# Sums of FFN weights formed in DRAM by accumulating transfers instead of by GpSimd in SBUF

## The chip, the cores and the metric

One core of one Trainium2 chip runs the program alone. The metric is device time in microseconds (us). The kernel before takes 1333.62 us, the median of three runs that lie between 1332.47 and 1334.59. The profile below is of one more execution, which took 1331.28 us.

## The reference, cut to what matters

Everything is float32. A decoder block of 1024 tokens and width 1024 computes two branches (sliding-window attention and an mLSTM), merges them, and then runs the feed-forward network (FFN), whose inner width is 2816. The change is in the FFN:

```python
x = x + (sigmoid(ga) * ya + sigmoid(gm) * ym) @ w_out     # branches, merged
f = rmsnorm(x, norm2_g)
x = x + (silu(f @ w_ffn_gate) * (f @ w_ffn_up)) @ w_ffn_down
return rmsnorm(x, final_norm_g)
```

w_ffn_gate and w_ffn_up are 1024 x 2816, w_ffn_down is 2816 x 1024.

## The kernel before

**Products in parts.** TensorE multiplies float32 as three passes over rounded halves: an operand is split into a rounded part `hi` (ScalarE copy) and the rest `lo` (VectorE subtraction), the helper `split` (L72, L73), and a product is hi·hi + hi·lo + lo·hi. A `whi` or `wlo` tile is such a half of a weight block of 128x512; five of each rotate.

**Seven products for eight.** The three matrix products of the FFN are cut into 2x2 blocks and done with the seven products of the Strassen-Winograd scheme. Products 1, 2 and 4 take a block of the weight as it is; products 5, 6, 7 and 3 take the sums x21+x22, x21+x22+x11, x11+x21 and x12+(x21+x22+x11) (the signs are folded into the other operand). `ORDER` and `SEQ` (L784 to L787) list the gate and up products: n runs over 22 panels (11 pairs of gate and up), i over the seven products, and each product is 12 matmuls of 128x512. In the projection down (`DORD`, L949) the seven products run one after the other, each over 11 chunks p of 12 matmuls.

**Where the sums are made.** `load_pair` brings a panel's raw blocks x11, x12, x21, x22 from `w_gu` by SP's queue; `prep` (L806 to L826) has GpSimd add two of them into a tile `s_` where product i needs a sum (L813) and splits it. `prep` runs LA = 4 products ahead of TensorE. In the projection down `dprep` (L981 to L998) does the same with tiles `lz` that `dload` has brought; GpSimd adds into `sT` or into the right half of `ld`, and for products 5 and 6 ScalarE copies `sT` into `ld`. The left half of `ld` is a combination of hidden activations (`hd_` in DRAM, stored by `h_store`).

**What sets the order.** Instructions of one engine run in the order in which the framework put them; DMAs are issued by SP's queue, also in order, so that a DMA which waits for a buffer or for data holds all that stand behind it. GpSimd (POOL) also makes one half of the activation sums `f_t` (L768), the activation `w` (L921) and the sums `hs` of hidden activations (L877).

**Stages in time.** Branches up to about 327 us; the attention projection (`w_br`, L665 to L668, result `mg`) from there; the mLSTM output gates (`sg`, L676 to L683); the merge; the projection `w_out` (j = 0 to 7, 12 us each, from 561 us); gate and up from 657 us; down until the end.

Of the kernel before, what the change touches and what calls it, by code (L numbers as in the profile page):

```python
# [9 lines left out]
F32 = mybir.dt.float32  # L10
F32R = mybir.dt.float32r
AF = mybir.ActivationFunctionType
ALU = mybir.AluOpType
PSUM = bass.MemoryType.PSUM

P = 128
S = 1024
D = 1024
FF = 2816
KD = D // P  # L20
NF = FF // P
NT = S // P
HALF = 512
EPS = 1e-6
# [5 lines left out]


@with_exitstack
def hybrid_block(ctx, tc, xT, xt, par, g3row, cst, abias, w_fm, w_mv, w_br, w_o, w_gu, w_dn, out):
    nc = tc.nc
    V, A, G, T = nc.vector, nc.scalar, nc.gpsimd, nc.tensor

# [4 lines left out]
    wp = ctx.enter_context(tc.tile_pool(name="wp", bufs=1))  # L41
    wk = ctx.enter_context(tc.tile_pool(name="wk", bufs=3))
    sm = ctx.enter_context(tc.tile_pool(name="sm", bufs=2))
# [7 lines left out]
    def blk(name, dtype=F32, n=1024):  # L51
        return sb.tile([P, n], dtype, name=name, tag="blk", bufs=NB)
# [18 lines left out]
    def split(hi, lo, src, eng=V):  # L71
        A.activation(hi, src, AF.Copy)  # L72
        eng.tensor_tensor(lo, src, hi.bitcast(F32), ALU.subtract)  # L73
# [40 lines left out]
    def hs(h):  # L114
        return slice(h * HALF, (h + 1) * HALF)
# [62 lines left out]
    for k in range(KD):  # L178
        xr = xrs[k]
        h_, l_ = blk("uh", F32R), blk("ul", F32R)  # L180
        g = prm[:, C_G1 + k:C_G1 + k + 1]
# [238 lines left out]
    mg = []  # L420
# [212 lines left out]
    run(gai, 16)  # L633


    ph_a.close()
    lo_eng[0] = V
    ph_b = ExitStack()
# [24 lines left out]
    for j in range(KD):  # L663
        wt = weights(w_br[j], 4)
        A.activation(mg[j], mg[j], AF.Sigmoid)  # L665
        for h in range(2):
            ps = proj(wt, o_, 4, h)
            V.tensor_tensor(mg[j][:, hs(h)], ps, mg[j][:, hs(h)], ALU.mult)  # L668


    hs_ = [[None, None], [None, None]]
    for i in range(4):
        wt = weights(w_fm[18 + i], KD)
        for h in range(2):
            if i % 2 == 0:
                hs_[h][i // 2] = (pv2(blk2("hh", F32R)), pv2(blk("hl", F32R)))  # L676
            sg = work("sg")
            gate(sg, wt, h)
            for q in range(2):
                V.scalar_tensor_tensor(sg[:, q * 256:(q + 1) * 256],  # L680
                                       hT[h * 2 + q][:, i * 256:(i + 1) * 256], prm[:, C_GM + i:C_GM + i + 1],
                                       sg[:, q * 256:(q + 1) * 256], ALU.mult, ALU.mult)
            hi, lo = (b[:, i % 2] for b in hs_[h][i // 2])  # L683
            split(hi, lo, sg)
    h_ = lambda k, h: tuple(b[:, k % 2] for b in hs_[h][k // 2])

# [65 lines left out]
    def halves(t):  # L752
        return t[:, 0:HALF], t[:, HALF:1024]
# [17 lines left out]
    def half(name, tag, bufs):  # L771
        return pC.tile([P, HALF], F32, name=name, tag=tag, bufs=bufs)
# [9 lines left out]


    ORDER = (1, 6, 5, 7, 2, 3, 4)  # L784
    NP2 = NF // 2
    SEQ = [(n, i) for i2 in ((1, 5), (6, 7), (2, 3, 4)) for n in range(2) for i in i2]
    SEQ += [(n, i) for n in range(2, 2 * NP2) for i in ORDER]  # L787
    LA = 4
    raws, hl, sums = {}, {}, {}

    def load_pair(n):

        raws[n] = [x for i in range(2) for x in pair_raw(n, i)]

    def pair_raw(n, i):
        if n == 0 and i == 1:
            r = [half("wr", "ev", 6) for _ in range(2)]
            for k in range(2):
                nc.sync.dma_start(out=r[k], in_=w_gu[n, i, :, hs(k)])
            return r  # L800
        r = blk("wr2") if i else wp.tile([P, 1024], F32, name="wraw", tag="wraw", bufs=2)
        nc.sync.dma_start(out=r, in_=w_gu[n, i])
        return halves(r)

    def prep(g):
        n, i = SEQ[g]  # L806
        if n and i == 6 and n + 1 < 2 * NP2:
            load_pair(n + 1)
        x11, x12, x21, x22 = raws[n]

        def s_(k, a, b):
            sums[n, k] = half("s_", "ws", 5)
            G.tensor_tensor(sums[n, k], a, b, ALU.add)  # L813
        if i in (5, 6) and (n, 5) not in sums:
            s_(5, x21, x22)
        if i == 6:
            s_(6, sums[n, 5], x11)
        elif i == 7:
            s_(7, x11, x21)
        elif i == 3:  # L820
            s_(3, x12, sums[n, 6])
        src = {1: x11, 2: x12, 4: x22}
        hi = wp.tile([P, HALF], F32R, name="whi", tag="whi", bufs=5)
        lo = wp.tile([P, HALF], F32R, name="wlo", tag="wlo", bufs=5)
        split(hi, lo, src[i] if i in src else sums[n, i])
        hl[n, i] = (hi, lo)  # L826

    later = []
    for j in range(KD):
        wt = weights(w_o[j], KD)  # L830
        xr = wp.tile([P, 1024], F32, name="xr2", tag="wraw", bufs=2)
        nc.sync.dma_start(out=xr, in_=xT[j])
        xc = blk("xc")
        f = blk("f")
        F_.append(f)
        g = prm[:, C_G2 + j:C_G2 + j + 1]
        if j == KD - 1:
            load_pair(0)
            prep(0)
            prep(1)  # L840
        for h in range(2):
            ps = proj(wt, m_, KD, h)
            V.tensor_tensor(xc[:, hs(h)], ps, xr[:, hs(h)], ALU.add)
            A.activation(f[:, hs(h)], xc[:, hs(h)], AF.Copy, scale=g)
            later.append((xc, j, h))
            if len(later) > 1:
                to_tokens(*later.pop(0))
        if j % 2 == 1 and j < 6:
            f_even(j // 2)
        elif j == 6:  # L850
            f_split(1, 3, F_[6][:, 0:HALF])
# [81 lines left out]
            if i == 4 and s == 1:  # L933
                h_sums(n // 2, sg)

    load_pair(1)

    def f_rest(i, kt):
        (z11, z12), (z21, z22) = halves(F_[2 * kt]), halves(F_[2 * kt + 1])
# [9 lines left out]
    DORD = (1, 5, 2, 3, 6, 7, 4)  # L949
    NC_ = 7 * NP2  # L950
    LD, LP = 6, 4
    draw, dop, sT, dtm = {}, {}, {}, {}

    def t_at(p):
        if (p // 2) not in sT:
            sT[p // 2] = blk("sT")
        return halves(sT[p // 2])[p % 2]

    def dload(c):

        i, p = DORD[c // NP2], c % NP2
        t = blk("ld")
        draw[c] = t
        nc.sync.dma_start(out=t[:, 0:HALF], in_=hd_[i - 1, p])

        def ld(k, j, dst=None):
            dst = half("lz", "ev", 6) if dst is None else dst
            nc.sync.dma_start(out=dst, in_=w_dn[2 * p + k, :, hs(j)])
            return dst
        z = t[:, HALF:1024]  # L970
        if i in (1, 2, 3):
            ld(*{1: (0, 0), 2: (1, 0), 3: (1, 1)}[i], z)
        elif i == 5:
            dtm[c] = ld(0, 0), ld(0, 1)
        elif i == 7:
            dtm[c] = ld(1, 1), ld(0, 1)
        elif i == 6:
            dtm[c] = (ld(1, 1),)
        else:
            dtm[c] = (ld(1, 0),)  # L980

    def dprep(c):
        i, p = DORD[c // NP2], c % NP2
        t = draw.pop(c)
        z, tm = t[:, HALF:1024], dtm.pop(c, None)
        if i == 5:
            G.tensor_tensor(t_at(p), *tm, ALU.add)
            A.activation(z, t_at(p), AF.Copy)
        elif i == 6:
            G.tensor_tensor(t_at(p), tm[0], t_at(p), ALU.add)  # L990
            A.activation(z, t_at(p), AF.Copy)
        elif i == 7:
            G.tensor_tensor(z, *tm, ALU.add)
        elif i == 4:
            G.tensor_tensor(z, tm[0], t_at(p), ALU.add)
        hi, lo = blk("xzh", F32R), blk("xzl", F32R)
        split(hi, lo, t)
        dop[c] = hi, lo  # L998

    z11, z12 = halves(F_[6])  # L1000
# [2 lines left out]
        f_rest(6, kt)  # L1003
    prep(2)
    prep(3)
    rest = [(i, kt) for i in (7, 2, 3, 4) for kt in range(4)]
    for g, (n, i) in enumerate(SEQ):
        if g + LA < len(SEQ):
            prep(g + LA)
        product7(n, i)  # L1010
        if g == 0:
            to_tokens(*later.pop(0))
            V.tensor_tensor(rstd2, ss2[:, 0], ss2[:, 1], ALU.add)
            rstd_of(rstd2, rstd2, D, NT)
        if n == 2 * NP2 - 1 and i in (7, 2, 3):
            for c in {7: range(LP), 2: range(2), 3: range(2, LP)}[i]:
                (dload if i == 7 else dprep)(c)
        for _ in range(2):
            if rest:
                f_rest(*rest.pop(0))  # L1020
# [95 lines left out]
def _layout(i):  # L1116
# [30 lines left out]
    def cols(w):  # L1147

        K, N = w.shape
        return np.ascontiguousarray(w.reshape(K // P, P, N // P, P).transpose(2, 1, 0, 3)).reshape(N // P, P, K)  # L1150
# [9 lines left out]
    w_br = np.concatenate([cols(wa), cols(a["w_mlstm_branch"][0])], axis=0)  # L1160
    w_o = cols(a["w_out"][0])

    w_gu = np.stack([cols(a[k][0]).reshape(NF // 2, 2, P, 4, 2, P).transpose(0, 1, 2, 4, 3, 5).reshape(NF // 2, 2, P, D)
                     for k in ("w_ffn_gate", "w_ffn_up")], axis=1).reshape(NF, 2, P, D)
    w_dn = a["w_ffn_down"][0].reshape(NF, P, D)
    return [xT, x.reshape(NT, P, D), par, np.tile(a["final_norm_g"][None, :], (P, 1)), cst, abias, w_fm, w_mv, w_br, w_o, w_gu, w_dn]


_NAMES = ["xT", "xt", "par", "g3row", "cst", "abias", "w_fm", "w_mv", "w_br", "w_o", "w_gu", "w_dn"]


# [15 lines left out]
```

## Time and profile before

| | |
|---|---|
| median of three runs | 1333.62 us |
| profiled execution | 1331.28 us |
| its span | 1329.5 us |
| TensorE busy | 1303.4 us (98%) |
| VectorE busy | 765.0 us (58%) |
| ScalarE busy | 572.7 us (43%) |
| GpSimd busy | 458.5 us (34%) |
| moved by DMA | 143.13 MB, mean 108 GB/s |

Engines: PE is TensorE, DVE VectorE, ACT ScalarE, POOL GpSimd, SPq the queue of DMAs that SyncE issues. A row of the chain or of a timeline names line, engine, operation, output and inputs, and behind a bracket the idle time ahead of it and what ended it. "PEclk" is the clock that TensorE was granted as a share of full speed (2.4 GHz; the other level is 1.2 GHz). A row for several instructions in a timeline ("x2") gives the time from the start of the first to the end of the last.

### The profile page before, as it was taken

To read this page: it belongs to the slowest core of one execution; us is meant where nothing else is said; L and a number is where in the kernel's file an instruction comes from. 1 tells how busy PE (TensorE), PEld (TensorE's weight loads), DVE (VectorE), ACT (ScalarE), POOL (GpSimd) and SP (SyncE) were. 2 spreads that over 40 slices of the span, in tenths; PEclk is the share of its full clock that TensorE was granted. 3 is DMA by queue.
4 is the path that set the end of the run, shared out by engine and by line. 5 is a ranking of instruction groups with operands and counts; after the bars stand their busy time and mean duration, and the time that the engine had idled before them with its cause. 6 is when DMAs were issued, how large, how long until landed. Compare 5 with 4: busy or idle time off the path is not lost.

```text
span 1329.5 us, 16764 instructions
## 1 busy us (share of the span) xinstructions
PE 1303.4 (98%) x6090; PEld 1066.1 (80%) x6090; DVE 765.0 (58%) x1261; ACT 572.7 (43%) x1078; POOL 458.5 (34%) x374
## 2 busy tenths in 40 slices
PE   8999999999999999999989999999999999999986
PEld 6888998777888888888778888888888888888865
DVE  5369764565535444433587555555556564664796
ACT  6369974566213222224453333333233344565333
POOL 0245443211000000010266657556655725600470
PEclk9999999999999999999989999999999999999989
DMA  9111011101111111224323321323232249983761
GB/s 338 48 57 39 17 33 48 49 9 33 56 48 42 44 48 49 73 64 158 121 67 121 119 97 71 103 103 119 104 119 82 85 168 309 331 287 92 261 230 64
DMA packets 61860, 143.13 MB, mean 108 GB/s; under 512 B 6992, under 2 KB 7248, under 8 KB 61776
## 3 DMA queue, kind: packets, MB, share of 16 engines
q1 hardware_dynamic: 61776, 142.05, 31.7%
q8 instruction: 48, 0.79, 0.2%
q14 instruction: 36, 0.29, 0.1%
HBM read 113.45 MB, written 28.57 MB: 107 GB/s over the span
## 4 chain that ended last, share of the span: by engine, by line
PE 87%; DVE 7%; issue 2%; ACT 1%; DMA 1%; POOL 1%; SPq 0%; DVEq 0%; POOLq 0%; ACTq 0%
PE mm L108 8%; PE mm L110 7%; PE mm L109 7%; PE mm L856 6%; PE mm L857 6%; PE mm L855 6%; PE mb L856 5%; PE mb L857 5%; PE mb L855 5%; PE st L857 4%; PE st L855 4%; PE st L856 4%; PE mb L110 4%; PE mb L109 4%; PE mb L108 4%
## 5 line engine op out<-in xcount | busy, mean ns | idle before, releaser
L72 ACT ACTIVATE whi<-wraw 128x512 fp32r<-128x512 f32 (+1 forms) x144 | 89.3, 628 | 221.3 <-PE mb L109 99.8
L73 DVE TENSOR_TENSOR xzl<-ld,xzh 128x1024 fp32r<-128x1024 f32 x77 | 110.4, 1463 | 69.3 <-ACT xzh L72 62.0
L108 PE MATMUL mm<-uh,whi 128*128 128x512 f32 x352 | 140.0, 400 | 1.1 <-ACT whi L72 1.1
L110 PE MATMUL mm<-uh,wlo 128*128 128x512 f32 x352 | 139.0, 395 | 0.0
L109 PE MATMUL mm<-ul,whi 128*128 128x512 f32 x352 | 138.7, 395 | 0.0
L73 DVE TENSOR_TENSOR wlo<-wraw,whi 128x512 fp32r<-128x512 f32 (+1 forms) x116 | 88.6, 771 | 76.4 <-ACT whi L72 75.5
L72 ACT ACTIVATE xzh<-ld 128x1024 fp32r<-128x1024 f32 x77 | 79.7, 1056 | 58.5 <-DMA ld<-in_w_dn_dram 24.9
L857 PE MATMUL mb<-z,wlo 128*128 128x512 f32 x220 | 87.8, 399 | 1.8 <-DVE wlo L73 1.8
L856 PE MATMUL mb<-z,whi 128*128 128x512 f32 x220 | 87.7, 399 | 0.0
L855 PE MATMUL mb<-z,whi 128*128 128x512 f32 x220 | 87.7, 399 | 0.0
L855 PE MATMUL mm<-z,whi 128*128 128x512 f32 x220 | 86.7, 394 | 0.0
L857 PE MATMUL mm<-z,wlo 128*128 128x512 f32 x220 | 86.7, 394 | 0.0
L856 PE MATMUL mm<-z,whi 128*128 128x512 f32 x220 | 86.7, 394 | 0.0
L813 POOL TENSOR_TENSOR s__5671<-wr 128x512 f32<-128x512 f32 x1 | 1.5, 1538 | 232.9 <-DMA wr<-in_w_gu_dram 232.9
L108 PEld LDWEIGHTS mm<-uh,whi 128*128 128x128 f32 x352 | 66.3, 188 | 17.0 <-ACT whi L72 2.3
L921 POOL TENSOR_TENSOR w<-w,d 128x512 f32<-128x512 f32 x22 | 36.0, 1636 | 126.7 <-DVE w L920 122.9
L110 PEld LDWEIGHTS mm<-uh,wlo 128*128 128x128 f32 x352 | 66.2, 188 | 15.6 <-DVE wlo L73 0.2
L109 PEld LDWEIGHTS mm<-ul,whi 128*128 128x128 f32 x352 | 66.3, 188 | 14.4
L857 PE MATMUL st<-z,wlo 128*128 128x512 f32 x176 | 69.4, 394 | 0.0
L855 PE MATMUL st<-z,whi 128*128 128x512 f32 x176 | 69.4, 394 | 0.0
L856 PE MATMUL st<-z,whi 128*128 128x512 f32 x176 | 69.2, 393 | 0.0
L890 ACT ACTIVATE sg<-sg 128x512 f32<-128x512 f32 x44 | 27.7, 629 | 88.1 <-DVE sg L889 49.9
(591 smaller groups left out, 3431.1 us busy)
## 6 DMA issues: line engine op xcount, KB each, us to landing
ld<-hd__5018 SPq DMA_DIRECT2D x77, 256.0 KB, 4.7
lz<-in_w_dn_dram SPq DMA_DIRECT2D x66, 256.0 KB, 4.9
wraw<-in_w_fm_dram SPq DMA_DIRECT2D x28, 512.0 KB, 3.5
wraw<-in_w_gu_dram SPq DMA_DIRECT2D x22, 512.0 KB, 3.6
hd__5018<-hs SPq DMA_DIRECT2D x44, 256.0 KB, 2.1
wr<-in_w_gu_dram SPq DMA_DIRECT2D x21, 512.0 KB, 6.0
hd__5018<-sg SPq DMA_DIRECT2D x33, 256.0 KB, 2.3
ld<-in_w_dn_dram SPq DMA_DIRECT2D x33, 256.0 KB, 5.2
```

The lines of the kernel that those rows point to most:

```text
L72: A.activation(hi, src, AF.Copy)
L73: eng.tensor_tensor(lo, src, hi.bitcast(F32), ALU.subtract)
L108: T.matmul(ps, ah, bh, start=(i == 0), stop=False)
L109: T.matmul(ps, ah, bl, start=False, stop=False)
L110: T.matmul(ps, al, bh, start=False, stop=(i == n - 1))
L813: G.tensor_tensor(sums[n, k], a, b, ALU.add)
L855: T.matmul(ps, xh, zh, start=start, stop=False, skip_group_check=more)
L856: T.matmul(ps, xh, zl, start=False, stop=False, skip_group_check=more)
L857: T.matmul(ps, xl, zh, start=False, stop=stop, skip_group_check=more)
L890: A.activation(dst, dst, AF.Silu)
L921: G.tensor_tensor(e["w"], e["w"], e["d5"], ALU.subtract)
```

## The change

The raw blocks are laid out in DRAM by kind (`wx[0..3]` are all x11, x12, x21 and x22 of gate and up, `wd[0..3]` those of down), and the four sums are formed there as whole arrays: `wS` for gate and up, `wT` for down. GpSimd issues 24 transfers of 352 rows of 8 KB (2.88 MB each): 12 copy an array from DRAM to DRAM, and 12 add an array to what lies at the destination. The 16 for gate and up are issued one by one, each behind a one-column copy by GpSimd (`token`) of a result: eight of `mg`, eight of `sg`. The eight for down are issued one behind each of the first eight panels of gate and up. The FFN then loads one block of 128x512 per product (`load`, LL = 4 products ahead of `prep`), raw or sum; GpSimd has no weights left to add, and ScalarE no `sT` to copy.

```diff
+    def add_up(x, s, groups):
+        x11, x12, x21, x22 = x
+        for steps in (((0, x21, 0), (2, x11, 0)), ((0, x22, 1), (2, x21, 1)), ((1, s[0], 0),), ((1, x11, 1),),
+                      ((3, s[1], 0),), ((3, x12, 1),)):
+            for k, src, add in steps:
+                for r in groups:
+                    if add:
+                        G.dma_start(out=s[k][r], in_=src[r], accum_op=ALU.add, max_dma_last_dim=8192)
+                    else:
+                        G.dma_start(out=s[k][r], in_=src[r], max_dma_last_dim=8192)
+                    yield
+    def paced(it, n, after):
+        token = sm.tile([P, 1], F32, name="token")
+        with tc.issue_after(G.tensor_copy(token, after[:, 0:1]).ins):
+            run(it, n)
+    ffn_sums = add_up([wx[b] for b in range(4)], wS, [slice(0, NP2 * 32), slice(NP2 * 32, NF * 32)])
+    down_sums = add_up([wd[b] for b in (3, 2, 1, 0)], wT, [slice(0, NP2 * 32)])
...
             V.tensor_tensor(mg[j][:, hs(h)], ps, mg[j][:, hs(h)], ALU.mult)
+        paced(ffn_sums, 1, mg[j])
...
+            paced(ffn_sums, 1, sg)
             split(hi, lo, sg)
...
-    def load_pair(n):
-        raws[n] = [x for i in range(2) for x in pair_raw(n, i)]
+    LL = 4
+    raw_of = {1: wx[0], 2: wx[1], 4: wx[3], 5: wS[0], 6: wS[1], 7: wS[2], 3: wS[3]}
+    def load(g):
+        if g < len(SEQ):
+            n, i = SEQ[g]
+            raws[g] = half("wo", "wo", 5)
+            nc.sync.dma_start(out=raws[g], in_=wblock(raw_of[i], n))
     def prep(g):
-        def s_(k, a, b):
-            sums[n, k] = half("s_", "ws", 5)
-            G.tensor_tensor(sums[n, k], a, b, ALU.add)
...
-        split(hi, lo, src[i] if i in src else sums[n, i])
+        split(hi, lo, raws.pop(g))
...
     def dload(c):
...
+        nc.sync.dma_start(out=t[:, HALF:1024], in_=wblock(z_of[i], p))
     def dprep(c):
-        if i == 5:
-            G.tensor_tensor(t_at(p), *tm, ALU.add)
-            A.activation(z, t_at(p), AF.Copy)
-        elif i == 6:
-            G.tensor_tensor(t_at(p), tm[0], t_at(p), ALU.add)
-            A.activation(z, t_at(p), AF.Copy)
-        elif i == 7:
-            G.tensor_tensor(z, *tm, ALU.add)
-        elif i == 4:
-            G.tensor_tensor(z, tm[0], t_at(p), ALU.add)
         hi, lo = blk("xzh", F32R), blk("xzl", F32R)
-        split(hi, lo, t)
+        split(hi, lo, draw.pop(c))
...
         product7(n, i)
+        if i == 4 and n < 10:
+            paced(down_sums, 1, sgs[n][2])
```

The order of TensorE's instructions is that of before. On POOL, around the start of gate and up, the kernel before has these rows (`f` is an activation sum, `s_` a weight sum, `rstd` the second norm):

```order
L768 TENSOR_TENSOR f<-f 128x512 x6
L813 TENSOR_TENSOR s__5786<-wr_5760 128x512
L813 TENSOR_TENSOR s__5792<-s__5671,wraw 128x512
L813 TENSOR_TENSOR s__5845<-wraw,wr 128x512
L813 TENSOR_TENSOR s__5878<-s__5786,wraw 128x512
L813 TENSOR_TENSOR s__5905<-wraw,wr_5760 128x512
L813 TENSOR_TENSOR s__5956<-wraw,s__5792 128x512
L813 TENSOR_TENSOR s__6054<-wraw,s__5878 128x512
L141 TENSOR_TENSOR rstd_5757<-rstd_5757,nhalf 128x8
L768 TENSOR_TENSOR f<-f 128x512
L813 TENSOR_TENSOR s__6116<-wr_5876 128x512
L768 TENSOR_TENSOR f<-f 128x512
```

At the same place POOL of the changed kernel has the last transfers for gate and up, and then these rows (`wS_3564` is the array of product 3):

```order
L656 COPY token<-sg 128x1
L650 DMA wS_3564<-wS_3562 352x2048
L656 COPY token<-sg 128x1
L648 DMA wS_3564<-in_w_x_dram 352x2048
L656 COPY token<-sg 128x1
L648 DMA wS_3564<-in_w_x_dram 352x2048
L797 TENSOR_TENSOR f<-f 128x512 x6
L142 TENSOR_TENSOR rstd_5813<-rstd_5813,nhalf 128x8
L797 TENSOR_TENSOR f<-f 128x512 x2
```

The eight weight sums between the activation sums are gone, and all 16 transfers stand ahead of the first activation sum.

On SP's queue, in the projection `w_out`, the changed kernel has these rows with the semaphores they wait for (DMASW are those of POOL's transfers: DMASW4 there is of the fifth transfer, DMASW2 at its second use of the eleventh; `wS_3561` and `wS_3562` are the arrays of products 5 and 6):

```order
L841 DMA xr_5167<-in_xT_dram 128x1024 [waits DMAHW4_49,DVE_49]
L829 DMA wo<-in_w_x_dram 128x512 [waits PE_49]
L829 DMA wo<-wS_3561 128x512 [waits DMASW4_49]
L829 DMA wo<-in_w_x_dram 128x512
L829 DMA wo<-wS_3561 128x512
L829 DMA wo<-wS_3562 128x512 [waits DMASW2_49]
L82 DMA wraw<-in_w_o_dram 128x1024 [waits DMAHW3_49,DVE_49]
```

Five loads of FFN operands, three of them of sums, stand ahead of the load of w_out's third block; before, two loads of raw blocks (L799) stood there.

## Rows read from the trace of the kernel before

**Rows 1.** The page: busy time, share and count of each engine.

```profile
PE 1303.4 (98%) x6090; PEld 1066.1 (80%) x6090; DVE 765.0 (58%) x1261; ACT 572.7 (43%) x1078; POOL 458.5 (34%) x374
```

**Rows 2.** The waits of PE: who waited for whom, us in all, times, longest.

```profile
PE mb L856 <- DVE xzl L73: 3.9, 2, 3.1
PE mm L146 <- DVE v L916: 3.4, 1, 3.4
...
PE mm L856 <- DVE xzl L73: 2.2, 1, 2.2
PE mb L857 <- DVE wlo L73: 1.8, 1, 1.8
```

**Rows 3.** Windows of PE: stretch, its length, busy, count, clock, DMA share, GB/s.

```profile
664.00:672.00 8.00, 6.17 (x21) 0.79 0.55 194
680.00:688.00 8.00, 6.21 (x28) 0.79 0.21 66
700.00:880.00 180.00, 180.00 (x779) 1.00 0.32 110
1260.00:1285.00 25.00, 21.11 (x79) 0.86 0.80 285
1295.00:1305.00 10.00, 7.77 (x34) 1.00 0.00 0
```

**Rows 4.** Window of DVE: stretch, its length, busy, count, clock, DMA share, GB/s.

```profile
658.00:681.00 23.00, 23.00 (x32) 0.93 0.41 138
```

**Rows 5.** Timeline of DVE at the start of gate and up: start, duration, instruction.

```profile
664.04 1.75 DVE L73 TENSOR_TENSOR wlo<-wraw,whi 128x512 fp32r<-128x512 f32 x1
...
676.39 1.78 DVE L768 TENSOR_TENSOR f<-f 128x512 f32<-128x512 f32 x1
...
680.97 0.68 DVE L916 TENSOR_TENSOR v<-mm,v 128x512 f32<-128x512 f32 x1
```

**Rows 6.** Timeline of POOL in the same stretch.

```profile
662.03 1.53 POOL L813 TENSOR_TENSOR s__5878<-s__5786,wraw 128x512 f32<-128x512 f32 x1 [2.61 <-DMA wraw<-in_w_gu_dram]
...
663.52 1.71 POOL L813 TENSOR_TENSOR s__5905<-wraw,wr 128x512 f32<-128x512 f32 x1
...
675.88 1.74 POOL L813 TENSOR_TENSOR s__6116<-wr 128x512 f32<-128x512 f32 x1
```

**Rows 7.** Timeline of DVE, POOL and SP near the end of down.

```profile
1265.21 3.46 DVE L1057 SCALAR_TENSOR_TENSOR xo<-xo,ss,g 128x512 f32<-128x512 f32 x2 [0.44 <-POOL ss L1054]
...
1288.47 3.49 DVE L1043 SCALAR_TENSOR_TENSOR xo<-e,rstd,xo 128x512 f32<-128x512 f32 x2
...
1296.71 1.41 DVE L1043 SCALAR_TENSOR_TENSOR xo<-e,rstd,xo 128x512 f32<-128x512 f32 x2
...
1279.32 13.79 POOL L995 TENSOR_TENSOR ld<-lz,sT 128x512 f32<-128x512 f32 x7 [0.38 <-issue]
...
1255.72 8.15 SPq L1058 DMA_DIRECT2D out_dram<-xo  x6
```

**Rows 8.** Windows again: the busiest stretch for DMA, and the branches.

```profile
345.00:581.00 236.00, 236.00 (x1024) 1.00 0.17 51
1140.00:1170.00 30.00, 30.00 (x132) 1.00 0.94 344
```

**Rows 9.** DMA issues: sizes, median us from issue to landing.

```profile
hd__5018<-hs SPq DMA_DIRECT2D x44, 256.0 KB, 2.1
...
wraw<-in_w_br_dram SPq DMA_DIRECT2D x16, 256.0 KB, 2.7
```

**Rows 10.** Timelines of DVE, POOL, SP and PE: the first result waited for, and the deadlines.

```profile
345.00 0.69 DVE L668 TENSOR_TENSOR mg<-mb,mg 128x512 f32<-128x512 f32 x1 [2.09 <-PE mb L110]
...
582.14 1.28 POOL L768 TENSOR_TENSOR f<-f 128x512 f32<-128x512 f32 x1 [15.31 <-DVE z L73]
...
573.63 0.33 SPq L81 DMA_DIRECT2D wraw<-in_w_o_dram  x1
...
597.18 0.48 PE L108 MATMUL mm<-mh,whi 128*128 128x512 f32 x1
```

More of the change, by code (lines that the diff above doesn't have):

```diff
@@ L21 @@
 NF = FF // P
+NP2 = NF // 2
 NT = S // P
@@ L32, in hybrid_block @@
 @with_exitstack
-def hybrid_block(ctx, tc, xT, xt, par, g3row, cst, abias, w_fm, w_mv, w_br, w_o, w_gu, w_dn, out):
+def hybrid_block(ctx, tc, xT, xt, par, g3row, cst, abias, w_fm, w_mv, w_br, w_o, wx, wd, out):
     nc = tc.nc
@@ L633, in hybrid_block @@
     run(gai, 16)
+    wS = [dr.tile([NF * 32, 2048], F32, name=f"wS{k}") for k in range(4)]
+    wT = [dr.tile([NP2 * 32, 2048], F32, name=f"wT{k}") for k in range(4)]
+    def add_up(x, s, groups):
[15 more added lines that the diff above has]
+    down_sums = add_up([wd[b] for b in (3, 2, 1, 0)], wT, [slice(0, NP2 * 32)])
     ph_a.close()
@@ L784, in hybrid_block @@
     ORDER = (1, 6, 5, 7, 2, 3, 4)
-    NP2 = NF // 2
     SEQ = [(n, i) for i2 in ((1, 5), (6, 7), (2, 3, 4)) for n in range(2) for i in i2]
@@ L788, in hybrid_block, with wblock @@
     LA = 4
-    raws, hl, sums = {}, {}, {}
-    def load_pair(n):
-        raws[n] = [x for i in range(2) for x in pair_raw(n, i)]
[L795 to L803, printed above, removed]
-    def prep(g):
[L806 to L809, printed above, removed]
-        def s_(k, a, b):
-            sums[n, k] = half("s_", "ws", 5)
-            G.tensor_tensor(sums[n, k], a, b, ALU.add)
[L814 to L817, printed above, removed]
-        elif i == 7:
[L819 to L822, printed above, removed]
+    raws, hl = {}, {}
+    LL = 4
+    def wblock(w, n):
+        return w[n * 32:(n + 1) * 32].rearrange("r (b c) -> (r b) c", c=HALF)
+    raw_of = {1: wx[0], 2: wx[1], 4: wx[3], 5: wS[0], 6: wS[1], 7: wS[2], 3: wS[3]}
[4 more added lines that the diff above has]
+            nc.sync.dma_start(out=raws[g], in_=wblock(raw_of[i], n))
+    def prep(g):
         hi = wp.tile([P, HALF], F32R, name="whi", tag="whi", bufs=5)
         lo = wp.tile([P, HALF], F32R, name="wlo", tag="wlo", bufs=5)
-        split(hi, lo, src[i] if i in src else sums[n, i])
-        hl[n, i] = (hi, lo)
+        split(hi, lo, raws.pop(g))
+        hl[SEQ[g]] = (hi, lo)
     later = []
@@ L837, in hybrid_block @@
         if j == KD - 1:
-            load_pair(0)
+            for g_ in range(LL):
+                load(g_)
             prep(0)
@@ L934, in product7 @@
                 h_sums(n // 2, sg)
-    load_pair(1)
+    for g in range(LL, 7):
+        load(g)
     def f_rest(i, kt):
@@ L951, in hybrid_block @@
     LD, LP = 6, 4
[L952 to L957, printed above, removed]
+    draw, dop = {}, {}
+    z_of = {1: wd[0], 2: wd[2], 3: wd[3], 5: wT[0], 6: wT[1], 7: wT[2], 4: wT[3]}
     def dload(c):
         i, p = DORD[c // NP2], c % NP2
-        t = blk("ld")
-        draw[c] = t
+        draw[c] = t = blk("ld")
         nc.sync.dma_start(out=t[:, 0:HALF], in_=hd_[i - 1, p])
[L966 to L976, printed above, removed]
-        elif i == 6:
-            dtm[c] = (ld(1, 1),)
-        else:
-            dtm[c] = (ld(1, 0),)
-    def dprep(c):
-        i, p = DORD[c // NP2], c % NP2
-        t = draw.pop(c)
-        z, tm = t[:, HALF:1024], dtm.pop(c, None)
-        if i == 5:
-            G.tensor_tensor(t_at(p), *tm, ALU.add)
-            A.activation(z, t_at(p), AF.Copy)
-        elif i == 6:
-            G.tensor_tensor(t_at(p), tm[0], t_at(p), ALU.add)
-            A.activation(z, t_at(p), AF.Copy)
-        elif i == 7:
-            G.tensor_tensor(z, *tm, ALU.add)
-        elif i == 4:
-            G.tensor_tensor(z, tm[0], t_at(p), ALU.add)
+        nc.sync.dma_start(out=t[:, HALF:1024], in_=wblock(z_of[i], p))
+    def dprep(c):
         hi, lo = blk("xzh", F32R), blk("xzl", F32R)
-        split(hi, lo, t)
+        split(hi, lo, draw.pop(c))
         dop[c] = hi, lo
@@ L1005, in hybrid_block @@
     prep(3)
+    load(7)
     rest = [(i, kt) for i in (7, 2, 3, 4) for kt in range(4)]
     for g, (n, i) in enumerate(SEQ):
+        load(g + LA + LL)
         if g + LA < len(SEQ):
@@ L1161, in _layout @@
     w_o = cols(a["w_out"][0])
[L1163 to L1169, printed above, removed]
+    w_x = np.stack([cols(a[k][0]).reshape(NP2, 2, P, 4, 2, P).transpose(1, 4, 0, 2, 3, 5).reshape(4, NP2, P, HALF)
+                    for k in ("w_ffn_gate", "w_ffn_up")], axis=2).reshape(4, NF * 32, 2048)
+    w_d = np.ascontiguousarray(a["w_ffn_down"][0].reshape(NP2, 2, P, 2, HALF).transpose(1, 3, 0, 2, 4)).reshape(4, NP2 * 32, 2048)
+    return [xT, x.reshape(NT, P, D), par, np.tile(a["final_norm_g"][None, :], (P, 1)), cst, abias, w_fm, w_mv, w_br, w_o, w_x, w_d]
+_NAMES = ["xT", "xt", "par", "g3row", "cst", "abias", "w_fm", "w_mv", "w_br", "w_o", "w_x", "w_d"]
 def kernel(**inputs):
```

## The prediction

> **What bounds the kernel now.** I read the page first. PE is busy 98% of the span [rows 1], so the change, which leaves PE's instructions and their order alone, can only win back PE's gaps, or open new ones. The waits of PE come next: nearly all that it waits for behind the branches is VectorE (DVE), at two places, 1.8 and 3.4 us at the start of gate and up and 3.9 and 2.2 us near the end of down [rows 2]. The windows then tell what a gap costs beyond itself. In an undisturbed stretch 779 instructions take 180 us, 0.231 us each. In 664 to 672 us and 680 to 688 us the granted clock is 0.79 (the engine had just stood still; it runs part of the window at 1.2 instead of 2.4 GHz), 0.21 x 8 us = 1.7 us each [rows 3]. The loss at the start of gate and up is thus 1.8 + 3.4 + 2 x 1.7 = 8.6 us. Near the end I count instructions: 1260 to 1285 us holds 79 where 25 / 0.231 = 108 fit, 29 x 0.231 = 6.7 us lost, clock included; 1295 to 1305 us holds 34 of 43, 2.1 us [rows 3]. All that can be won is 8.6 + 6.7 + 2.1 = 17.4 us.
>
> Last, the timeline of DVE says why it is late there. From 658 us until it delivers `v` at 681 us it has no pause [rows 4], and its instructions of one size take either 0.68 us or 1.75 to 1.78 us [rows 5]. The long ones lie over a weight sum on POOL: the `wlo` at 664.04 over the sum at 663.52, the `f` at 676.39 over that at 675.88 [rows 5, 6]. A sum on POOL costs DVE about 1.1 us. Near the end, two `xo` take 3.46 and 3.49 us where POOL is adding and 1.41 us where it isn't [rows 7].
>
> **What the change removes.** All weight sums on POOL, with ScalarE's copies of `sT`; POOL and ScalarE themselves are far from bounding (34% and 43%) [rows 1], so what counts is DVE's time beside them. At the start of gate and up, five weight sums lie over DVE's work between 662.03 and 677.6 us (the first two and the last are shown) [rows 6]; at 1.1 us each, `v` comes about 5.5 us sooner. The `wlo` at 664.04 lies behind the first sum and over the second, so it ends about 2 us sooner, against a wait of 1.8 us: this gap goes, with its 1.7 us of slow clock. Without it PE wants `v` 3.5 us sooner still, 3.4 + 3.5 = 6.9 us ahead of now, and gets it 5.5 us ahead: some 1.4 us of wait stay, and perhaps a little slow clock. I take 6.5 of the 8.6 us. Near the end, POOL's adds lie over the two long `xo` (2 us each) and over the `xzl` of 1279 to 1293 us [rows 7]. There the other cause stays: six stores of the output hold SP's queue for 8 us at 1255.72 while they wait for DVE [rows 7], and the loads of the next operands stand behind them. They are freed as DVE gets done, about 3 us sooner. I take 5 of the 6.7 us and all of the 2.1 us. The gain is 6.5 + 5 + 2.1 = 13.6 us. Nothing is won between 700 and 1250 us, since PE has no gap there.
>
> **What it adds on engines.** 24 `token` copies and 24 issues on POOL. Neither is in the trace. A DVE instruction beside one of them loses at most the 1.1 us that it loses beside a sum, 26 us of DVE's time if all 24 collide, but they stand in stretches where PE doesn't wait for DVE [rows 2]. On PE's path I bound them by 0 and 3 us (three collisions), and take 1.5.
>
> **What it adds on the DMA queues.** Each transfer moves 2.88 MB. The trace has no transfer from DRAM to DRAM and none that adds. Rates for bounds: 344 GB/s at a DMA share of 0.94, so 366 GB/s in full [rows 8]. If reading and writing go on at once, a copy takes 2.88 MB / 366 GB/s = 7.9 us, and an add, if its two reads also went at once, the same; if each pass has the engines to itself, a copy takes 15.8 us and an add 23.6 us. Made of single 256 KB pieces one after the other, each loaded (2.7 us) and stored (2.1 us) [rows 9], a copy would take 11 x 4.8 = 53 us, which I take for no end, because one large transfer keeps all engines queued as in the 344 GB/s stretch and doesn't pay the landing of each piece. That stretch is the nearest row, so copy 7.9 us, and for the add 15.8 us, two reads in turn.
>
> The first transfer waits for `mg` at 345.7 us. POOL has to issue all 16 before its first activation sum, at 582.14 us [rows 10]; the 16th waits for the 14th to land. The loads there take 0.17 of the DMA engines [rows 8]. Eight copies and six adds end at 345.7 + (8 x 7.9 + 6 x 15.8) / 0.83 = 536 us, in time. The five operand loads that stand ahead of the load of w_out's third block (573.63 us before) need the 11th transfer (six copies and five adds): 345.7 + 126 / 0.83 = 498 us, in time as well. Weight loads of the branches, 2.7 us to landing [rows 9], become slower beside the transfers, but two raw buffers and five halves put them 10 us and more ahead. So the branches cost nothing in my forecast.
>
> The Trainium skill has a rule on the price of the add (Collectives: The Full Stack, section The bandwidth ceiling): an add reads two sources through the same ring and so runs at half the rate of a copy. With it the add is twice the copy, as taken; without it (7.9 us) the 14th transfer would land at 479 us, and the time of the kernel would be the same; no row here shows which.
>
> In gate and up, each product now loads 256 KB, 94 GB/s at 12 x 0.231 us, and the stores of `hd_` (seven of 256 KB in two panels, 38.8 us) add 47: 141 GB/s, 0.39 of the engines, where before it was 0.32 [rows 3]. The eight transfers for down come one per panel (19.4 us) and need 4 x 7.9 + 4 x 15.8 = 95 us of 155 us, 0.61: just all of it. In down itself a chunk loads 512 KB instead of up to 768 KB, so its peaks, 344 GB/s [rows 8], go.
>
> **The sum.** 13.6 - 1.5 = 12 us less. From the profiled execution (span 1329.5 us, 1331.3 us with what lies around it) that gives 1319 us; the median of the runs shown, 1333.6, is 2.3 us above that execution, so I predict 1322 us, with 1314 (nearly all 17.4 us and 2 us of scatter) to 1328 (half) as its own range.
>
> **Rivals.**
> *The sums come late (slower).* Place: POOL's queue and ScalarE behind it. If the 14th transfer lands later than about 590 us, the activation sum of 582 us is late, ScalarE waits for it in its own order, and the halves of w_out's block j = 3 behind it miss PE's first use at 597.18 us [rows 10]; ScalarE has about 10 us to spare there. With an add of two copies this decides at 20 p / 0.83 = 244 us, a copy of p = 10.1 us or 285 GB/s. At the upper ends, 15.8 and 23.6 us, the 14th lands at 345.7 + 268 / 0.83 = 669 us, a stop of about 80 us, 1400 us in all; with 12 and 20 us at 606 us, 16 us and a slow clock, 1340 us. For it: nothing in the trace shows these rates. Against: the nearest row gives 50 us to spare. The Trainium skill (DMA: Bandwidth & Descriptors, section Latency and other measured facts) gives 207 to 214 GB/s for copies between tensors in HBM; by that figure, as an estimate, a copy takes 13.7 us and, doubled, an add 27 us, the 14th lands near 675 us and the kernel takes about 1405 us; no run here shows it yet.
>
> *The sums for down crowd the FFN's loads.* 0.39 + 0.61 leaves no room. If an engine takes pieces of both queues in turn, each 8 KB piece of an add (0.72 us, 22 per engine) lets one 2 KB piece of a load through, 0.7 MB during an add where gate and up wants 2.5 MB. It falls 13 us behind per add; two adds follow each other, and a load leads its product by nine products, 25 us less landing. Two gaps of about 4 us with 1.7 us of slow clock, and stores that hold SP's queue, make it 1322 + 11 = 1333 us, 1328 to 1345.
>
> *The gaps stay.* DVE is not late through POOL alone but through its place in line and the stores in SP's queue; then 1329 to 1333 us, 1331. Against: the long and short durations of one instruction.
>
> **Chances.** Forecast 0.55; late sums 0.18; crowded loads 0.17; gaps stay 0.10. What this kernel's times can tell from no change is 0.2%, 2.7 us. Faster by more: the forecast, 0.04 of crowded loads and 0.02 of gaps that stay, 0.61. Within: 0.07 of each of these two, 0.14. Slower: 0.18 and the rest, 0.25. The range of 1314 to 1346 leaves out 0.05 below and most of the late sums above.
>
> **What would show it.** Right: no sum of weights on POOL; `wlo` and `xo` at 0.7 us each; PE's waits for `v`, `wlo` and `xzl` below 3 us in all; full clock through 660 to 690 us. The landing of the transfers for gate and up before 580 us shows the rates. Wrong: ScalarE waiting for POOL's `f` near 583 us, PE waiting for `whi` in w_out, SP's queue waiting on POOL's transfers, or PE waiting for `wlo` in panels 2 to 8.

## The result and the profile after

The changed kernel takes 1397.38 us (median of 4 runs, 1394.59 to 1398.37), the kernel before 1333.25 us in the same sitting: 1.0477 times as long, with a 95% interval of [1.0458, 1.0495]. I had said 1322 us, so the forecast was wrong in its sign. The profiled execution has a span of 1392.8 us, 63.3 us more than before.

The page of the kernel after shows where at first sight. It gives the span, busy time of each engine, and PE's busy share, TensorE's clock and the DMA share in 40 slices of 35 us:

```profile
span 1392.8 us, 16858 instructions
...
PE 1313.9 (94%) x6090; PEld 1069.4 (77%) x6090; DVE 700.2 (50%) x1261; ACT 557.8 (40%) x1056; POOL 277.0 (20%) x292
...
PE   9999999999994459999999999999999999999997
...
PEclk9999999999997679999999999999999999999999
DMA  9111001102988888613434899974445456855661
```

POOL's sums of weights are gone (34% busy [rows 1], now 20%), but PE falls from 98% to 94%. Its loss lies in the slices 13 to 15, some 420 to 520 us, in the stage of the output gates (`sg`), where before the change it never paused [rows 8]. To see what each stage did, I take from the lines of PE the first product of gate and up and the first of down (the last two numbers of a row's times are the first and last start):

```profile
L865 PE MATMUL mm<-z,whi x220: 387/394/478, 725.1 to 1150.0; 128*128 128x512 f32 x110
...
L865 PE MATMUL mm<-xzh x132: 387/393/421, 1170.1 to 1380.2; 128*128 128x512 f32 x132
```

With the same rows of each kernel (657.3 and 1097.0 us in the kernel before) the span falls into three parts. "Up to gate and up" holds the branches and w_out; the names in the last eight rows are those of the experiments below. Each row is one execution. A part of the first column is no effect of the transfers: the first gate of the branches (L416 before, L417 in the others), ahead of every transfer, starts anywhere from 213.0 to 216.4 us.

| kernel | up to gate and up, us | gate and up, us | down to the end, us | span, us |
|---|---|---|---|---|
| before | 657.3 | 439.7 | 232.5 | 1329.5 |
| after | 725.1 | 445.0 | 222.7 | 1392.8 |
| e1: token reads `hl` | 663.4 | 445.0 | 222.6 | 1331.0 |
| e2: own buffers for `sg` | 719.0 | 446.9 | 222.6 | 1388.5 |
| e3: three times the room | 698.6 | 446.0 | 223.1 | 1367.7 |
| e4: e1, down's transfers half as dense | 661.0 | 433.5 | 222.7 | 1317.2 |
| e5: e1, transfers for gate and up only | 661.4 | 431.7 | 233.8 | 1326.9 |
| e6: e1, down's transfers later | 658.6 | 442.9 | 222.5 | 1324.1 |
| e7: e4, four copies earlier | 658.1 | 432.8 | 222.7 | 1313.6 |
| e8: e4, transfers for down only | 659.7 | 440.5 | 222.9 | 1323.1 |

So after the change 67.8 us are lost before gate and up, 5.3 us in gate and up, and 9.8 us are won in down.

**The wait that wasn't there before.** The waits of PE after the change (us in total, times, longest):

```profile
PE mm L109 <- ACT whi L73: 20.7, 4, 14.1
PE mm L111 <- DVE wlo L74: 13.3, 1, 13.3
PE mb L109 <- ACT hh L73: 11.6, 1, 11.6
PE mm L109 <- ACT hh L73: 9.9, 1, 9.9
PE mb L865 <- ACT v L924: 5.9, 3, 2.2
...
PE mm L147 <- DVE v L926: 0.5, 1, 0.5
```

The waits of [rows 2] for DVE that I wanted gone are gone: `v` at the start of gate and up falls from 3.4 to 0.5 us, the FFN's `wlo` and `xzl` are no longer among the rows (the `wlo` of L111 is one of the branches). In their place PE waits for halves of weights and of `hs` in the branches. `whi` and `hh` are made by ScalarE, which is 40% busy: it must itself be waiting. What it waits for longest is DVE's `sg` (L417, 137.8 us in all), so the next view is the waits of DVE from 380 to 570 us:

```profile
DVE sg L417 <- POOL token L656: 103.5, 6, 35.9
```

and in its timeline (start, duration, in brackets the idle time before and what ended it):

```profile
399.93 0.69 DVE L417 TENSOR_TENSOR sg<-mm,Rt 128x512 f32<-128x512 f32 x1 [1.82 <-PE mm L111]
...
440.15 0.69 DVE L417 TENSOR_TENSOR sg<-mb,Rt 128x512 f32<-128x512 f32 x1 [35.90 <-POOL token L656]
...
536.72 0.69 DVE L417 TENSOR_TENSOR sg<-mm,Rt 128x512 f32<-128x512 f32 x1 [12.72 <-POOL token L656]
...
742.20 0.68 DVE L926 TENSOR_TENSOR v<-mm,v 128x512 f32<-128x512 f32 x1
...
1326.42 1.42 DVE L1039 SCALAR_TENSOR_TENSOR xo<-xo,ss,g 128x512 f32<-128x512 f32 x2 [0.47 <-POOL ss L1036]
```

The first three gates pass; the fourth stands 35.9 us for a `token` of POOL. The gate's `sg` is a work tile with three buffers that are used in turn, and the token copy is one of the readers of `sg`. The fourth gate wants the buffer of the first, and may have it when the first token has been copied. Why that is so late, POOL's timeline tells:

```profile
366.19 0.20 POOL L656 COPY token<-mg 128x1 f32<-128x1 f32 x1
385.35 1.02 POOL L648 DMA_DIRECT2D wS<-in_w_x_dram  x1 [18.96 <-DVE wlo L74]
...
403.41 0.95 POOL L648 DMA_DIRECT2D wS<-in_w_x_dram  x1 [16.85 <-issue]
...
422.29 0.94 POOL L648 DMA_DIRECT2D wS<-in_w_x_dram  x1 [17.74 <-issue]
...
438.99 0.94 POOL L648 DMA_DIRECT2D wS<-in_w_x_dram  x1 [15.57 <-issue]
439.57 0.54 POOL L656 COPY token<-sg 128x1 f32<-128x1 f32 x1
455.82 0.61 POOL L650 DMA_DIRECT2D wS<-wS  x1 [15.71 <-issue]
...
456.54 0.59 POOL L650 DMA_DIRECT2D wS<-wS  x1
...
478.05 0.97 POOL L648 DMA_DIRECT2D wS<-in_w_x_dram  x1 [20.72 <-issue]
...
554.85 0.96 POOL L648 DMA_DIRECT2D wS<-in_w_x_dram  x1 [18.17 <-issue]
650.03 1.28 POOL L797 TENSOR_TENSOR f<-f 128x512 f32<-128x512 f32 x1 [94.22 <-DVE z L74]
```

POOL works in order. L648 is the issue of an add, L650 that of a copy. From 385 us on POOL stands 15 to 21 us at ten of twelve issues, and "issue" says that it waits for nothing that the profile shows. (At the first the profile names a `wlo` of DVE; at the same place in e1 it names nothing, for 19.30 us.) The landings tell more: the add of 385.35 us lands 17.7 us after its issue, at 403.05, and the next is issued at 403.41; that one lands 18.6 us after, at 422.0, and the next is issued at 422.29. The token of the first gate, whose `sg` was done when the second gate's came at 394 us, is copied at 439.57 us, right behind the issue that held POOL; the gate of 440.15 us starts within 0.6 us of it. The windows of PE tell what this costs (width, busy time with instructions, granted clock, DMA share, GB/s):

```profile
420.00:560.00 140.00, 85.18 (x311) 0.79 0.85 213
```

The kernel before does 606 instructions in this window, at full clock. The 295 that are missing are, at 0.231 us each [rows 3], 68 us: all of the 67.8 us that the part before gate and up lost. The slow clock (0.79) is a part of it.

### The profile page after: what moved, and what is told of

The parts are those of the page before. It is cut to its first block, busy times and chain, and to the rows that moved or that the text cites. A ratio compares the mean times of both kernels' runs of the same rounds, so it can differ in the third digit from the quotient of the medians.

```text
span 1392.8 us, 16858 instructions
## 1 busy us (share of the span) xinstructions
PE 1313.9 (94%) x6090; PEld 1069.4 (77%) x6090; DVE 700.2 (50%) x1261; ACT 557.8 (40%) x1056; POOL 277.0 (20%) x292
## 4 chain that ended last, share of the span: by engine, by line
PE 72%; issue 14%; DVE 5%; DMA 5%; ACT 2%; POOL 2%; SPq 0%; POOLq 0%; DVEq 0%; ACTq 0%
PE mm L109 6%; PE mm L111 5%; PE mm L110 5%; PE mm L866 5%; PE mm L865 5%; PE mm L867 5%; PE mb L865 5%; PE mb L867 5%; PE mb L866 5%; PE st L865 4%; PE st L867 4%; PE st L866 4%; DMA wo<-wS 2%; PE mb L111 2%; PE mb L110 2%
## 5 line engine op out<-in xcount | busy, mean ns | idle before, releaser
L73 ACT ACTIVATE whi<-wo 128x512 fp32r<-128x512 f32 x154 | 96.4, 628 | 200.6 <-PE st L866 45.6
L74 DVE TENSOR_TENSOR wlo<-wo,whi 128x512 fp32r<-128x512 f32 x154 | 114.2, 746 | 97.0 <-ACT whi L73 97.0
L111 PE MATMUL mm<-uh,wlo 128*128 128x512 f32 x352 | 140.9, 400 | 13.3 <-DVE wlo L74 13.3
L74 DVE TENSOR_TENSOR xzl<-ld,xzh 128x1024 fp32r<-128x1024 f32 x77 | 92.9, 1243 | 78.8 <-ACT xzh L73 72.3
L73 ACT ACTIVATE whi<-wraw 128x512 fp32r<-128x512 f32 (+1 forms) x100 | 61.0, 626 | 131.1 <-PE mb L110 52.6
L109 PEld LDWEIGHTS mm<-uh,whi 128*128 128x128 f32 x352 | 67.5, 192 | 31.4 <-ACT whi L73 16.4
L111 PEld LDWEIGHTS mm<-uh,wlo 128*128 128x128 f32 x352 | 67.4, 192 | 29.9 <-DVE wlo L74 14.3
L74 DVE TENSOR_TENSOR wlo<-wraw,whi 128x512 fp32r<-128x512 f32 (+1 forms) x72 | 48.8, 689 | 57.9 <-ACT whi L73 57.9
L419 ACT ACTIVATE sg<-sg 128x512 f32<-128x512 f32 x24 | 15.1, 630 | 137.8 <-DVE sg L417 137.8
## 6 DMA issues: line engine op xcount, KB each, us to landing
wS<-wS POOLq DMA_DIRECT2D x4, 2816.0 KB, 16.4
```

The lines of the kernel that those rows point to most:

```text
L109: T.matmul(ps, ah, bh, start=(i == 0), stop=False)
L111: T.matmul(ps, al, bh, start=False, stop=(i == n - 1))
L419: A.activation(dst, dst, AF.Sigmoid)
```

## The experiments

Theory T1, formed from these rows: the token's read of `sg` ties the gates to POOL's queue; without it the branches run as before. The rivals: T2, the transfers themselves starve the branches, whose weights load beside them; T3, POOL's stands at its issues would hold PE in some other way. In the table above and below, gate and up has its own question: why it became 5.3 us longer instead of 6.5 us shorter.

**e1: the token reads another tile.** Same transfers and as many tokens. Only the eight tokens of the `hs` loop read the half that the split of `sg` has just made and that lasts to the end of the merge.

```diff
-            paced(ffn_sums, 1, sg)
             split(hi, lo, sg)
+            paced(ffn_sums, 1, lo.bitcast(F32))
```

> The eight tokens of the mLSTM gates read hl (a tile that stays until the merge) instead of sg (a tile of three that rotate); nothing else differs, on no engine. Theory T1: the tokens, which stand in POOL's queue behind transfers that it can't issue yet, keep sg's three buffers, DVE waits for POOL and PE for DVE; without that the 67 us lost between 420 and 560 us go, 1397 - 67 = 1330 us, and DVE no longer waits for POOL's token there. Rival T2: the transfers take the DMA engines from the weight loads of the branches, and ScalarE's halves are late through that; then the time stays at 1385 us or more. The transfers themselves run back to back from 342 to about 573 us under both.

Measured: 1331.95 us, 0.9975 of before [0.9964, 0.9986]. In the same window PE is never idle, with the transfers as dense as they were:

```profile
420.00:560.00 140.00, 140.00 (x605) 1.00 0.91 235
```

One operand of eight instructions is worth 65.4 us. POOL still stands at its issues (the 16th goes out at 569.37 us), and this alone costs PE nothing in that window. T1 holds, T2 and T3 fall as causes of the large loss. That the loads do suffer is seen in this view of DMA issues from 345 to 580 us (count, KB each, median us from issue to landing); before, the loads of 512 KB landed in 3.5 us:

```profile
wS<-in_w_x_dram POOLq DMA_DIRECT2D x12, 2816.0 KB, 18.4
wS<-wS POOLq DMA_DIRECT2D x4, 2816.0 KB, 18.0
wraw<-in_w_fm_dram SPq DMA_DIRECT2D x12, 512.0 KB, 10.0
```

**e2: more buffers for the same read.** The token reads `sg` as in the changed kernel, but the eight `sg` of the loop have three buffers of their own.

```diff
-            sg = work("sg")
+            sg = pB.tile([P, HALF], F32, name="sgx", tag="sgx", bufs=3)
```

> The tokens read sg as before, but the eight gates have three buffers of their own, so that the gates of the merge behind them rotate through others. T1: the last DVE instruction held is gate 7, by token 4 (495.8 us in the changed kernel, 427 us in its natural course), instead of gate 10 by token 7 (536.1 against 449.6); PE runs some 20 us ahead of a held gate, so about 49 us are lost instead of 67: 1379 us, within 6. T2: no change, 1397 us.

Measured: 1387.01 us, 1.0381 [1.0359, 1.0402]. It lies outside the 6 us that I had allowed. DVE's waits in the same stretch:

```profile
DVE sgx L417 <- POOL token L656: 76.1, 4, 35.9
```

Fewer gates wait (four instead of six), and the last gates of the stretch are released; the direction is T1's. The size is not: about 10 us saved instead of 18. I had counted on PE to make up some 20 us of a gate's delay. The last gate held starts at 499.74 us, 69 us later than in e1 (430.31), and the part before gate and up is 62 us longer than before the change, so PE made up less than 10.

**e3: POOL may have more transfers under way.** The program reserves room for the descriptors of POOL's transfers; it is tripled. One buffer of `hs` is given up for it.

```diff
-            t = half("hs", "hs", 3)
+            t = half("hs", "hs", 2)
...
-    nc = _bacc.Bacc(..., dynamic_dma_scratch_size=1024)
+    nc = _bacc.Bacc(..., dynamic_dma_scratch_size=3072)
```

> Three times the room for descriptors of POOL's transfers (3072 instead of 1024; to make room the activation sums hs have two buffers instead of three). If POOL stands because the room is full, the first adding transfer is issued near 367 us instead of 385, the tokens come earlier until the waits for landed transfers hold them (token 7 near 524 instead of 536 us), and the time falls by about 12 us to 1385. If POOL stands for landed transfers alone, no change, 1397 us.

Measured: 1368.13 us, 1.0247 [1.023, 1.0265], 17 us better than I said. The timeline of POOL:

```profile
367.24 0.99 POOL L648 DMA_DIRECT2D wS<-in_w_x_dram  x1 [0.27 <-issue]
...
388.48 0.94 POOL L648 DMA_DIRECT2D wS<-in_w_x_dram  x1 [4.75 <-DMA wS<-in_w_x_dram]
...
457.41 0.95 POOL L648 DMA_DIRECT2D wS<-in_w_x_dram  x1 [37.19 <-DMA wS<-wS]
...
513.08 0.94 POOL L648 DMA_DIRECT2D wS<-in_w_x_dram  x1 [7.99 <-DMA wS<-wS]
```

The stand at the first add is gone (issued at 367.24 instead of 385.35 us, after 0.27 us instead of 18.96), so the "issue" time there was a lack of room. From 388 us on POOL waits for something that the profile names: a transfer of the sums that has to land first, 37.19 us at 457.41. So room is only one of two reasons for a late token; the other is the order of the sums themselves. In e1 PE loses nothing to either from 420 to 560 us.

**e4: down's transfers on every second panel.** e1, and in gate and up the eight transfers for down go out on every second panel, 1 to 15 of the 22, instead of on the first eight.

```diff
-        if i == 4 and n < 10:
+        if i == 4 and n % 2 == 1:
```

> As e1, and the eight transfers for down are issued behind every second panel of gate and up, 38.8 us apart instead of 19.4. If their crowding of the FFN's loads costs the 11 us that PE loses between 800 and 960 us in the changed kernel, 1330 - 11 = 1319 us, and PE has no gap in gate and up; if the gaps come from the order of SP's queue or from POOL, 1330 us as e1.

Measured: 1320.28 us, 0.9891 [0.9875, 0.9907], as expected. Gate and up takes 433.5 us where e1 takes 445.0: what the dense transfers cost is 11.5 us. In e1's stage PE waits 7.3 us for ScalarE's `whi` and `v`, and from 760 to 840 us its granted clock is 0.96, another 3 us; in e4 1.2 us of such waits are left and the clock is 1.00. The landing of the operands' loads (L829) from 700 to 900 us, minimum, median and maximum, first e1, then e4:

```profile
DMA to landing us min/median/max: 2.5/8.3/17.4
```

```profile
DMA to landing us min/median/max: 2.4/3.4/18.4
```

The longest stays, the median does not. An estimate from POOL's rows above, 10.8 us for a copy and 17.9 us for an add (see the rates below), gives a likely reason: four copies and four adds need 115 us, of the 155 us that eight panels last, and of 310 us in e4. Over all of e4's gate and up PE is busy 431.84 of 433.50 us; the row is of a window that begins in it and runs on into down:

```profile
775.00:1240.00 465.00, 463.84 (x2001) 1.00 0.69 214
```

**e6: the same density, later.** To tell density from place: e1 with `if i == 4 and 8 <= n < 18:` in the same line.

> As e1, with the eight transfers for down one per panel again, but behind panels 8 to 15 instead of 0 to 7. If their density is what costs gate and up 11.5 us, the same gaps open in panels 9 to 16 and the time is that of e1, 1332 us. If it is the place (the first panels, their other loads), the gaps go: 1320 us as e4.

Measured: 1326.21 us, 0.994 [0.9927, 0.9952]. Gate and up takes 442.9 us, near e1's 445.0, and the slow landings have moved along (860 to 1040 us: median 9.5 us, in e1 2.8 us there). So it is density, not the place at the start. The total lies between my two numbers mainly because the part before gate and up took 658.6 us where e1 took 663.4, with the same instructions there. Of the 6.1 us that e1 is behind the kernel before in that part, 1.8 lie ahead of the first transfer (its first gate starts at 215.6 us, before the change at 213.8, in e6 at 213.7) and 3.9 in w_out: from the last merged `mg` (L730; L701 before) to gate and up it is 98.6 us in e1, 98.1 in e4, 95.7 in e6, and 94.7 in the kernel before and in the changed kernel. The waits of ScalarE from 540 to 605 us, of e1 and then of e7 (below), show w_out's loads late beside the last adds:

```profile
ACT whi L73 <- DMA wraw<-in_w_o_dram: 18.4, 3, 10.1
```

```profile
ACT whi L73 <- DMA wraw<-in_w_o_dram: 8.5, 3, 2.9
```

In e6 the longest of these waits is shorter than in e1, 7.3 us instead of 10.1, but their sum is larger, 23.6 us instead of 18.4. Why two kernels that are alike up to there differ by 2.9 us in w_out, no run tells.

**e5 and e8: one half of the change at a time.** In e5 the sums for gate and up are formed by transfers (with e1's token), those for down by POOL as before; in e8 it is the other way round (with e4's spacing). The core of e5's edit, and of e8's:

```diff
-        if i == 4 and n < 10:
-            paced(down_sums, 1, sgs[n][2])
...
+        if i == 5:
+            G.tensor_tensor(t_at(p), *tm, ALU.add)
+            A.activation(z, t_at(p), AF.Copy)
```

```diff
-    raw_of = {1: wx[0], 2: wx[1], 4: wx[3], 5: wS[0], 6: wS[1], 7: wS[2], 3: wS[3]}
...
+        def s_(k, a, b):
+            sums[n, k] = half("s_", "ws", 5)
+            G.tensor_tensor(sums[n, k], a, b, ALU.add)
```

> As e4, but the sums of down are made as in the kernel before, by GpSimd in SBUF with ScalarE's copies, and no transfer runs in gate and up. From the first product of gate and up, e4 takes 433.5 us for gate and up and 222.7 us for down; the kernel before 439.7 and 232.5. If the 9.8 us in down come from the sums that left POOL (DVE free of them, smaller loads), they are lost again: 1320 + 10 = 1330 us, with DVE's long xo and xzl and PE's gaps behind 1250 us back. If they come from something else in e4, 1320 us.

> The other half alone: the sums of down by transfers as in e4, those of gate and up by GpSimd as in the kernel before (from loads of 256 KB instead of 512 KB); no transfers in the branches. Branches as before (657 us), gate and up as before (439.7 us, with the gaps of its start), down as e4 (222.7 us): span 1319.4, 1322.5 us as a median. If the transfers crowd gate and up here too, up to 5 us more.

Measured: e5 1325.31 us, 0.9935 [0.992, 0.9951]; e8 1323.77 us, 0.9921 [0.9908, 0.9934]. The waits of PE name what comes back when POOL sums again, near the end in e5 and at the start of gate and up in e8:

```profile
PE mb L866 <- DVE xzl L74: 3.9, 2, 3.1
PE mm L866 <- DVE xzl L74: 3.6, 1, 3.6
```

```profile
PE mm L147 <- DVE v L946: 5.6, 1, 5.6
...
PE mb L887 <- DVE wlo L74: 1.1, 1, 1.1
```

Each gap of [rows 2] comes back with the sums of its own stage. Down takes 233.8 us to the end in e5 and 222.9 us in e8. e8's time is 1.3 us from the expected one. e5's down is as slow as I said, yet its median is 5 us below the 1330 us that I expected. Its six runs spread from 1322.02 to 1328.71 us, and the profiled one is the slowest of them; how much of the 5 us is scatter stays open. With POOL's adds e5 brings back ScalarE's copies and the larger loads of down too, so no run tells these three apart.

**e7: the best version.** e4, and the first four copies, which need no result of the branches, go out during the mLSTM loop ahead of them, one on every second of its steps; the `hs` loop then issues four of its eight transfers.

```diff
         if c > 0:
             ml_c(c - 1)
+        if c % 2:
+            paced(ffn_sums, 1, hT[c // 2])
...
-            paced(ffn_sums, 1, sg)
             split(hi, lo, sg)
+            if h:
+                paced(ffn_sums, 1, lo.bitcast(F32))
```

> As e4, but the first four transfers (copies) are issued in the mLSTM stage ahead, behind every second result of it, so that the others end some 40 us sooner, before w_out. If the 3 to 4 us that e4 still loses up to gate and up come from weight loads of w_out beside the last transfers, they go: 1316 us. If POOL stands for room at the copies and holds the small operations of the mLSTM, more than 1325 us.

Measured: 1315.2 us (1314.8 to 1316.93), 0.9863 [0.985, 0.9876], faster than both kernels. The last transfer of the sums for gate and up goes out at 520.57 us, in e4 at 564.56 and in e1 at 569.37. w_out's loads no longer lie beside it (longest wait 2.9 us, the rows above; 9.8 in e4), and PE does 185 instructions between 560 and 600 us, where e4 did 169 and e1 165 (PE's window of e7):

```profile
560.00:600.00 40.00, 40.00 (x185) 1.00 0.29 99
```

From the last merged `mg` to gate and up it is 94.7 us, as before the change: the 3.4 us that e4 lost there are back, of the 5.1 us by which e7 is faster than e4.

## Why the prediction was wrong

**The step that failed** is the one on the engines: "24 `token` copies and 24 issues on POOL", bounded "by 0 and 3 us" and taken at 1.5 us because "they stand in stretches where PE doesn't wait for DVE". I priced a token as work, by what it takes from a DVE instruction beside it. What it costs is the wait it makes: it reads `sg`, so it stands between a gate and the third gate behind it, and it stands in POOL's queue behind transfers that POOL can't issue. I had left unasked what needs the buffer that a token reads. In DVE's timeline the first three gates are released by PE, the fourth by the token. e1 prices the step at 65.4 us, where its bounds ended at 3. (The tokens are 26, not 24: the last two come behind panels 8 and 9 and pace no transfer.)

**The late sums** did not happen where that rival put them. I had the 14th transfer land at 536 us; it landed at 535.2 in the changed kernel (issued at 514.61, 20.6 us to landing) and at 548.7 in e1. All 16 were issued by 554.85 us, and POOL's first activation sum (650.03, the last row of its timeline) waited for DVE. The rival had the right queue (POOL's) and the wrong tenant: I followed only the sums behind the transfers, not the tokens. That its upper number, 1400 us, lies near the measured 1397 is chance. What the transfers did cost w_out, 3.9 us in e1, goes with late loads of its weights, not with late sums.

**The rates** of the sum were of the right kind and too high. Taken: a copy 7.9 us, an add 15.8 us. Two copies hold POOL for 21.5 us (456.54 to 478.05), about 10.8 us or 268 GB/s each; the issues of adds follow each other in 18.06, 18.88 and 16.70 us, 17.9 in the mean. The ratio is 1.7. The share of 0.83 that I left the transfers made up for it, 9.5 and 19.0 us, so the landing of the 14th came out. The Trainium skill (Collectives: The Full Stack, section The bandwidth ceiling) says of collectives that the one that adds runs at half the rate of the one that copies, for its two reads; the ratio here agrees in kind, and the 1.93 measured there is not reached. The Trainium skill (DMA: Bandwidth & Descriptors, section Latency and other measured facts) gives 207 to 214 GB/s for copies of tiles between HBM tensors at its better row pitches; the 268 GB/s of these copies lie above it, and the measurement decides.

**The crowded loads**, a rival at 0.17, happened: priced at 11 us, measured 11.5 us (e1 against e4). This is the forecast's second wrong term: by the estimate of e4 the transfers need 115 of 155 us, 0.74 of the engines and not 0.61, which with the 0.39 of the loads is more than there is. The place (760 to 840 us, panels 4 to 8) and the makeup, waits and a slower clock, are the rival's, though PE waited for ScalarE's `whi` and `v`, hardly for `wlo` (0.4 us); its picture of pieces taken in turn was not tested. With the token repaired, the change as written would have ended there: 1331.95 us, against the 1333 of that rival.

**The gains** were right in kind. The start of gate and up: `v`, `wlo` and the slow clock behind them gone; `v` comes 17.1 us behind the stage's first product (742.20 - 725.1), before 23.7 (680.97 - 657.3), 6.6 us sooner where I said 5.5. Gate and up takes 433.5 us in e4 against 439.7, and 431.7 in e5; I took 6.5. The end: 9.8 us, where I took 7.1 and counted only 8.8 as lost. DVE's `xo` takes 1.42 us there (3.46 before [rows 7]), and in down no wait of PE is left: the 1.7 us that I kept for the stores on SP's queue were not lost. e4 carries out the change with the token and the density mended and measures 1320 us, near the 1322 that I had forecast for the change itself. That is partly luck: it gains 16.0 us in the two stages where I took 13.6, and loses 3.4 us in w_out, where I had put nothing.

## What to carry to other kernels

An instruction that only paces another queue still reads a tile, and holds that tile's buffer until it has run: let it read something that lasts, never a tile whose buffers are used in turn. Before giving an in-order engine large transfers to issue, ask how many may be under way; behind the last of them the engine stands, and with it everything that waits for any small instruction in its queue. And a transfer that fits into the mean share of the DMA engines can still be too dense: spread over twice the time, the same eight transfers cost gate and up 1.8 us (433.5 us in e4, 431.7 without them in e5) instead of 13.

## What the hardware showed that I had not expected

- POOL stood 15 to 21 us at an issue, for a time in which the profile shows no wait; with three times the room for descriptors the first add was issued after 0.27 us. With the smaller room an add was issued within 0.4 us of the landing of the add before it (403.05 and 403.41, 422.0 and 422.29 us), and two copies went out together (455.82 and 456.54 us): the room held two copies or one add.
- An add of 2.88 MB from DRAM to DRAM took 16.4 to 19.0 us from issue to landing in the changed kernel; of two copies issued one behind the other (455.82 and 456.54 us) the first landed after 12.0 us and the second after 21.2.
- Loads of 512 KB beside such transfers landed in 10.0 us (e1, 345 to 580 us; 3.5 us before), and yet PE lost nothing from 420 to 560 us there. In gate and up single loads of 256 KB took up to 18.4 us (e4).
- DVE's instructions of 128x512 that took 1.75 us beside POOL's sums [rows 5] took 0.69 us while POOL stood at an issue (the gate of 399.93 us).
